# Gate and up projections of a SwiGLU layer by seven block products in place of eight

## The chip, the cores and the metric

The kernel runs on one core of a Trainium2 chip. The metric is the time of one execution on the device in microseconds (us); several executions are made and the median is taken.

## What is computed

Two layers of an encoder trunk, with the same weights for a batch of 512 tokens and one of 256, 768 tokens in all, of width 1024. Each layer has mixers (attention, retention, a recurrent group) and then the feed-forward part that this change touches. All of it is in float32:

```python
h = _rms(x, p['norm_ffn_pre'][l])
f = (jax.nn.silu(h @ p['ffn_w_gate'][l]) * (h @ p['ffn_w_up'][l])) @ p['ffn_w_down'][l]
x = x + _rms(f, p['norm_ffn_post'][l])
```

The inner width is D_FF = 2816, that is 22 feature tiles of 128.

## The kernel before

Every operand of a matmul is split into a high part (rounded to the matmul's format, float32r) and a low part, the rest. A product is then three matmuls: high by high, high by low, low by high. `hh` and `hl` hold the two parts of the normalised tokens, transposed: 8 blocks of 128 features by 768 tokens.

`piece` (L155) loads 128x1024 of weights into a `raw` buffer on SyncE's queue, writes the high part on ScalarE (L162) and the low part on VectorE or GpSimd in turn (L165). `feat_mm` (L181) multiplies the weights of one feature tile by a range of tokens: 8 blocks of the width by three matmuls (L189). Its columns are the tokens: 512 or 256.

`ffn` (L1239) goes through the 22 feature tiles in pairs (FFG = 2). For each tile `ffn_up` (L1189) makes the gate in the PSUM banks `pb` (`fg`) and the up projection in `pS` (`fu`), for both token ranges; tanh on ScalarE (L1197) and three steps on VectorE (L1198, L1217, L1220) give the activation, split into `ah` (L1219) and `al`. `ffn_down` (L1222) then takes both tiles at once: for each of six token tiles and two halves of the width, six matmuls of 512 columns into a `pa` bank (`dn`, L1231) and a sum into `y` on VectorE (L1237). The first pair goes by token ranges, and so does the last, whose down projection is followed tile by tile by the normalisation (`post_norm`, L218; `pre_norm`, L210, for the next layer).

All buffers come from pools with a tag and a fixed number of slots; a tile that finds no free slot waits until one is released:

```python
SLOTS = dict(raw=2, whi=3, wlo=3, E0=1, E1=1, E2=1, E3=1, E4=1, D=10, T=3, X=4, Z=2, z=2, V=2, Q=3, R=3, sm=2)
BANKS = dict(pa=2, pb=2, pS=2, pT=1, pO=1)
```

`R` slots hold 512 columns, `D` slots 768, `raw`, `whi`, `wlo` and `X` 1024. The order of the instructions on each engine is not the written one: a scheduler sets it when the program is built, by priority in the written order among what it finds ready. On the chip each engine then keeps that order and waits on semaphores.

Of the kernel before, what the change touches and what calls it, by code (L numbers as in the profile page):

```python
# [19 lines left out]
P = 128  # L20
L = 2
# [18 lines left out]
FFG = 2  # L40
# [18 lines left out]
FAST = (PIECE_D, PIECE_D + 2, PIECE_D + 6)  # L59
XM_TAG, XF_TAG = "ZXZXZX", "VZZVZZ"  # L60
# [22 lines left out]
class Trunk:  # L83
    def __init__(self, ctx, tc, xp, xs, wp, pv, bc, par, cst, scan, strips, yp, ys):
# [19 lines left out]
        self.nlo = 0  # L104
# [1084 lines left out]
    def ffn_up(self, l, f, seqs, wg, wu, th, ah, al):  # L1189
        nc = self.nc  # L1190
        part = len(seqs) < 2
        pg, pu = {}, {}

        def gate(s):
            t0, n, *_r = SEQS[s]
            c = slice(t0, t0 + n)
            nc.scalar.activation(th[:, c], pg[s][:, :n], AF.Tanh, scale=0.5)  # L1197
            nc.vector.scalar_tensor_tensor(out=th[:, c], in0=th[:, c], scalar=1.0, in1=pg[s][:, :n], op0=ALU.add, op1=ALU.mult)  # L1198

        for s in seqs:  # L1200
            pg[s] = self.bank("pS" if part else "pb", f"fg{l}_{f}_{s}")
            if not part:
                self.feat_mm(pg[s][:, :SEQS[s][1]], *wg, P, *SEQS[s][:2])
                gate(s)
        for s in seqs:
            t0, n, *_r = SEQS[s]
            c = slice(t0, t0 + n)
            pu[s] = self.bank("pS", f"fu{l}_{f}_{s}")
            if part:

                for a in range(0, n, 256):
                    self.feat_mm(pg[s][:, a:a + 256], *wg, P, t0 + a, 256)
                    self.feat_mm(pu[s][:, a:a + 256], *wu, P, t0 + a, 256)
                gate(s)
            else:
                self.feat_mm(pu[s][:, :n], *wu, P, t0, n)
            nc.vector.scalar_tensor_tensor(out=th[:, c], in0=th[:, c], scalar=0.5, in1=pu[s][:, :n], op0=ALU.mult, op1=ALU.mult)  # L1217
        c = slice(SEQS[seqs[0]][0], SEQS[seqs[-1]][0] + SEQS[seqs[-1]][1])
        nc.scalar.activation(ah[:, c], th[:, c], AF.Copy)  # L1219
        nc.vector.tensor_tensor(out=al[:, c], in0=th[:, c], in1=ah[:, c].bitcast(F32), op=ALU.subtract)  # L1220
# [18 lines left out]
    def ffn(self, l):  # L1239
# [4 lines left out]
        for f0 in range(0, NF, FFG):  # L1244
            fin = f0 + FFG >= NF
            tiles = [(self.tmp(f"th{l}_{f}"), self.slot("D", [P, TOK], f"ah{l}_{f}", F32R), self.slot("D", [P, TOK], f"al{l}_{f}", F32R))
# [209 lines left out]
```

## Time and profile before

| | |
|---|---|
| median of three runs (2332.1 to 2345.1) | 2338.31 us |
| profiled execution | 2336.97 us |
| its span, from the first to the last instruction | 2335.2 us |
| TensorE clock granted over the span, share of full | 0.979 |
| start of the first and the last gate matmul (`fg`) | 597.5 and 2307.6 us |
| start of the last down matmul (`dn`) of layer 0, of layer 1 | 1177.3 and 2324.5 us |
| DMA, mean over the span | 103 GB/s |

A row of a timeline has the start and the length in us, then the engine, the line and the operation with output<-inputs; in brackets stands how long the engine was idle before it, and what it waited for. PE is TensorE's matmul, PEld its weight load, DVE VectorE, ACT ScalarE, POOL GpSimd, SP SyncE. Matmuls overlap in their pipeline, so the distance of two starts, not the length, is what one costs in a row of them.

### The profile page before, as it was taken

To read this page: it belongs to the slowest core of one execution; us is meant where nothing else is said; L and a number is where in the kernel's file an instruction comes from. 1 tells how busy PE (TensorE), PEld (TensorE's weight loads), DVE (VectorE), ACT (ScalarE), POOL (GpSimd) and SP (SyncE) were. 2 spreads that over 40 slices of the span, in tenths; PEclk is the share of its full clock that TensorE was granted. 3 is DMA by queue.
4 is the path that set the end of the run, shared out by engine and by line. 5 is a ranking of instruction groups with operands and counts; after the bars stand their busy time and mean duration, and the time that the engine had idled before them with its cause. 6 is when DMAs were issued, how large, how long until landed. Compare 5 with 4: busy or idle time off the path is not lost.

```text
span 2335.2 us, 39824 instructions
## 1 busy us (share of the span) xinstructions
PE 2246.6 (96%) x15960; PEld 2028.8 (87%) x15960; DVE 1291.8 (55%) x2404; ACT 804.5 (34%) x1675; POOL 582.5 (25%) x521
## 2 busy tenths in 40 slices
PE   7999999999899999999999899999999999999997
PEld 7889999989888888888888799898898888888886
DVE  5598557885623333333567874678855343333345
ACT  4333335566431111221244333455654211222111
POOL 1342313325311111111233422133352111111113
PEclk9999999999999999999999899999999999999999
DMA  4543563335421111222324525633453111122112
GB/s 170 134 113 98 156 193 110 93 113 178 145 79 55 63 55 55 72 73 73 102 87 125 134 78 146 204 104 88 131 189 117 64 63 55 55 73 73 64 64 81
DMA packets 245080, 240.69 MB, mean 103 GB/s; under 512 B 138784, under 2 KB 191904, under 8 KB 244896
## 3 DMA queue, kind: packets, MB, share of 16 engines
q1 hardware_dynamic: 244896, 238.15, 33.2%
q8 instruction: 126, 2.06, 0.4%
q14 instruction: 58, 0.48, 0.1%
HBM read 183.03 MB, written 55.05 MB: 102 GB/s over the span
## 4 chain that ended last, share of the span: by engine, by line
PE 37%; DVE 7%; DMA 2%; issue 1%; ACT 1%; SPq 1%; POOL 1%; DVEq 0%; POOLq 0%; ACTq 0%
PE fg L189 8%; PE fu L189 8%; PE dn L1231 8%; PE dz L189 2%; PE op L178 2%; PE za L178 1%; PE zb L178 1%; PE pg L592 1%; DVE wlo L165 1%; PE px L575 1%; PE ob L766 1%; DMA raw<-in_wp_dram 1%; PE sd L537 1%; PE zc L178 1%; DVE nper L455 1%
## 5 line engine op out<-in xcount | busy, mean ns | idle before, releaser
L165 POOL TENSOR_TENSOR wlo<-raw,whi 128x1024 fp32r<-128x1024 f32 (+1 forms) x108 | 259.4, 2402 | 1034.9 <-ACT whi L162 854.7
L1237 DVE TENSOR_TENSOR y<-y,dn 128x512 f32<-128x512 f32 x240 | 162.7, 686 | 340.4 <-PE dn L1231 339.8
L162 ACT ACTIVATE whi<-raw 128x1024 fp32r<-128x1024 f32 (+1 forms) x222 | 225.3, 1021 | 334.3 <-DMA raw<-in_wp_dram 121.1
L189 PE MATMUL fg<-hh,whi 128*128 128x256 f32 (+1 forms) x768 | 250.4, 326 | 0.9 <-ACT hh L202 0.9
L189 PE MATMUL fg<-hl,whi 128*128 128x256 f32 (+1 forms) x768 | 250.4, 326 | 0.4 <-DVE hl L203 0.4
L189 PE MATMUL fg<-hh,wlo 128*128 128x256 f32 (+1 forms) x768 | 249.2, 325 | 0.0
L189 PE MATMUL fu<-hl,whi 128*128 128x256 f32 (+1 forms) x768 | 249.1, 324 | 0.0
L189 PE MATMUL fu<-hh,whi 128*128 128x256 f32 (+1 forms) x768 | 249.0, 324 | 0.0
L189 PE MATMUL fu<-hh,wlo 128*128 128x256 f32 (+1 forms) x768 | 248.4, 323 | 0.0
L165 DVE TENSOR_TENSOR wlo<-raw,whi 128x1024 fp32r<-128x1024 f32 (+1 forms) x114 | 154.6, 1356 | 128.8 <-ACT whi L162 127.8
L1231 PE MATMUL dn<-whi,ah 128*128 128x512 f32 x528 | 208.9, 396 | 1.9 <-DVE y L1237 1.9
L1231 PE MATMUL dn<-wlo,ah 128*128 128x512 f32 x528 | 209.4, 397 | 0.0
L1231 PE MATMUL dn<-whi,al 128*128 128x512 f32 x528 | 203.8, 393 | 0.0
L189 PEld LDWEIGHTS fg<-hh,whi 128*128 128x128 f32 x768 | 146.4, 191 | 16.1 <-ACT hh L202 1.3
L189 PEld LDWEIGHTS fg<-hl,whi 128*128 128x128 f32 x768 | 146.1, 190 | 15.1 <-DVE hl L203 1.0
L189 PEld LDWEIGHTS fu<-hl,whi 128*128 128x128 f32 x768 | 146.3, 190 | 13.6
L189 PEld LDWEIGHTS fu<-hh,wlo 128*128 128x128 f32 x768 | 146.1, 190 | 13.7
L189 PEld LDWEIGHTS fg<-hh,wlo 128*128 128x128 f32 x768 | 146.3, 190 | 13.4
L189 PEld LDWEIGHTS fu<-hh,whi 128*128 128x128 f32 x768 | 146.4, 191 | 13.1
L1219 ACT ACTIVATE ah<-th 128x768 fp32r<-128x768 f32 (+2 forms) x52 | 38.6, 742 | 297.6 <-DVE th L1217 297.6
L1197 ACT ACTIVATE th<-fg 128x512 f32<-128x512 f32 (+1 forms) x88 | 42.7, 485 | 234.8 <-PE fg L189 234.2
L1231 PEld LDWEIGHTS dn<-whi,al 128*128 128x128 f32 x528 | 98.7, 188 | 23.3
(358 smaller groups left out, 5586.6 us busy)
## 6 DMA issues: line engine op xcount, KB each, us to landing
raw<-in_wp_dram SPq DMA_DIRECT2D x184, 512.0 KB
raw<-in_wp_dram SPq DMA_DIRECT2D x38, 384.0 KB
kr<-kd SPq DMA_DIRECT2D x96, 64.0 KB
kr<-kd SPq DMA_DIRECT2D x48, 128.0 KB
x<-xm SPq DMA_DIRECT2D x24, 256.0 KB
xf<-x SPq DMA_DIRECT2D x12, 512.0 KB
gain<-in_bc_dram SPq DMA_DIRECT2D x8, 512.0 KB
bd<-sh SPq DMA_DIRECT2D x8, 512.0 KB
```

What stands on the lines that cost most here:

```text
L162: nc.scalar.activation(hi[:, :n], raw[:, :n], AF.Copy)
L165: eng.tensor_tensor(out=lo[:, :n], in0=raw[:, :n], in1=hi[:, :n].bitcast(F32), op=ALU.subtract)
L178: mm(ps, lhsT=a, rhs=b[:, c:c + ncol], start=i == 0, stop=i == tot - 1)
L189: mm(ps, lhsT=a, rhs=b, start=i == 0, stop=i == 3 * NK - 1)
L455: V.tensor_tensor(out=q[:, j + 1:32, 0:j], in0=q[:, j + 1:32, 0:j], in1=ev, op=ALU.add)
L537: T.matmul(psv[h][:, d, q], lhsT=bks[d][H[h], q], rhs=krs[d][H[h], h, q], start=True, stop=True)
L575: T.matmul(pxv[:, u], lhsT=krs[d][:, h, q], rhs=svs[d][:, h, q], start=True, stop=True)
L592: T.matmul(pgv[:, u], lhsT=brs[d][:, h, q], rhs=svs[d][:, h, q], start=True, stop=True)
L1197: nc.scalar.activation(th[:, c], pg[s][:, :n], AF.Tanh, scale=0.5)
L1219: nc.scalar.activation(ah[:, c], th[:, c], AF.Copy)
L1231: nc.tensor.matmul(ps, lhsT=a[p], rhs=w[q], start=i == 0, stop=i == tot - 1)
L1237: nc.vector.tensor_tensor(out=yt, in0=yt, in1=ps, op=ALU.add)
```

## The change

The first pair of feature tiles stays as it was, except that its down projection comes after both token ranges. For the other ten pairs of a layer, gate (and then up) of two feature tiles by 1024 by 768 tokens is seen as a 2x2 block product: the weights have two feature tiles by two halves of the width, the tokens two halves of the width by two halves of 384 tokens. Seven products of weight sums and token sums (Winograd's form of Strassen's product) take the place of eight block products, each of 4 blocks by three matmuls with 384 columns.

`ffn_sums` makes the token sums T1 to T4 once a layer, split into high and low parts, in buffers that other stages leave free (`TS_TAGS`); T1 overwrites a quarter of `hh` and `hl`. `block_weights` loads the two weight pieces, splits the first (w0) and the lower half of the second (w2, in `R`), lets GpSimd make four sums in place in `raw`, and splits these (wb, wa). `block_products` runs the seven products and adds them up on VectorE and GpSimd, with copies on ScalarE. `ffn_pair` does this for gate and up and makes the activation. The down projection of a pair is written behind the next pair's products, and that of the last pair comes after all, with its weights in `whi` and `wlo`.

```diff
-FFG = 2
+HT = TOK // 2
...
+TS_TAGS = ("Q", "T", "T", "T", "Z", "Z", "V", "D", "D", "Q", "Q")
...
-    def ffn_up(self, l, f, seqs, wg, wu, th, ah, al):
...
+    def ffn_sums(self, l):
+
+        nc = self.nc
+        V, S, A = nc.vector, nc.scalar, nc.gpsimd
+        F = lambda x: x.bitcast(F32)
+        L, R = slice(0, HT), slice(HT, TOK)
+        units = [self.slot(tag, [P, 2, HT], f"ts{l}_{i}", F32R) for i, tag in enumerate(TS_TAGS)]
+        cells = [u[:, j] for u in units for j in range(2)]
+        cells += [self.slot("z", [P, HT], f"tz{l}_{i}", F32R) for i in range(2)]
+        t1s = [self.tmp(f"t1{l}_{j}").rearrange("p (k c) -> p k c", k=2) for j in range(2)]
+        self.tt = {}
+        for k in range(4):
+            t1 = t1s[k // 2][:, k % 2]
+            t2, t3, t4 = [self.slot("R", [P, 512], f"t{n}{l}_{k}")[:, :HT] for n in (2, 3, 4)]
+            for eng, o, r, c in ((A, t1, k, L), (A, t3, k, R), (V, t2, 4 + k, R), (V, t4, 4 + k, L)):
+                eng.tensor_tensor(out=o, in0=F(self.hh[:, r, c]), in1=F(self.hl[:, r, c]), op=ALU.add)
+            A.tensor_tensor(out=t1, in0=t3, in1=t1, op=ALU.subtract)
+            A.tensor_tensor(out=t3, in0=t2, in1=t3, op=ALU.subtract)
+            V.tensor_tensor(out=t2, in0=t2, in1=t1, op=ALU.subtract)
+            V.tensor_tensor(out=t4, in0=t2, in1=t4, op=ALU.subtract)
+            for n, x in ((2, t2), (3, t3), (4, t4)):
+                hi, lo = cells.pop(0), cells.pop(0)
+                S.activation(hi, x, AF.Copy)
+                V.tensor_tensor(out=lo, in0=x, in1=F(hi), op=ALU.subtract)
+                self.tt[n, k] = hi, lo
+        for k in range(4):
+            t1, hi = t1s[k // 2][:, k % 2], self.hh[:, k, R]
+            S.activation(hi, t1, AF.Copy)
+            V.tensor_tensor(out=self.hl[:, k, R], in0=t1, in1=F(hi), op=ALU.subtract)
+
+    def block_h(self, n, k):
+
+        if n in (2, 3, 4):
+            return self.tt[n, k]
+        row, c = {1: (k, slice(HT, TOK)), "11": (k, slice(0, HT)), "21": (4 + k, slice(0, HT)), "22": (4 + k, slice(HT, TOK))}[n]
+        return self.hh[:, row, c], self.hl[:, row, c]
+
+    def block_mm(self, name, w, n):
+
+        mm = self.nc.tensor.matmul
+        ps = self.bank(("pb", "pb", "pS", "pS", "pT", "pO")[self.nbank % 6], name)[:, :HT]
+        self.nbank += 1
+        i = 0
+        for k in range(4):
+            wh, wl = [x[:, k * P:(k + 1) * P] for x in w]
+            bh, bl = self.block_h(n, k)
+            for a, b in ((wh, bh), (wh, bl), (wl, bh)):
+                mm(ps, lhsT=a, rhs=b, start=i == 0, stop=i == 11)
+                i += 1
+        return ps
+
+    def block_weights(self, l, f, i):
+
+        nc = self.nc
+        V, S, A = nc.vector, nc.scalar, nc.gpsimd
+        F = lambda x: x.bitcast(F32)
+        H = slice(0, 512), slice(512, 1024)
+        raw = []
+        for j in range(2):
+            r = self.slot("raw", [P, 1024], f"raw{l}_{f + j}_{i}")
+            nc.sync.dma_start(out=r, in_=self.wp[l, PIECE_FF + 3 * (f + j) + i])
+            raw.append(r)
+        a, b = raw
+        nm = f"{l}_{f}_{i}"
+
+        def split(hi, lo, x):
+            S.activation(hi, x, AF.Copy)
+            V.tensor_tensor(out=lo, in0=x, in1=F(hi), op=ALU.subtract)
+            return hi, lo
+
+        pair = lambda n: [self.slot(tag, [P, 1024], f"w{n}{nm}_{j}", F32R) for j, tag in enumerate(("whi", "wlo"))]
+        w0 = split(*pair("a"), a)
+        w2 = split(*[self.slot("R", [P, 512], f"w{n}2{nm}", F32R) for n in "hl"], b[:, H[1]])
+
+        A.tensor_tensor(out=b[:, H[1]], in0=b[:, H[0]], in1=b[:, H[1]], op=ALU.add)
+        A.tensor_tensor(out=b[:, H[0]], in0=a[:, H[0]], in1=b[:, H[0]], op=ALU.subtract)
+        A.tensor_tensor(out=a[:, H[0]], in0=b[:, H[1]], in1=a[:, H[0]], op=ALU.subtract)
+        A.tensor_tensor(out=a[:, H[1]], in0=a[:, H[1]], in1=a[:, H[0]], op=ALU.subtract)
+        wb = split(*pair("c"), b)
+        wa = split(*pair("b"), a)
+        part = lambda w, j: tuple(x[:, H[j]] for x in w)
+        return {"A11": part(w0, 0), "A12": part(w0, 1), "A22": w2, "S1": part(wb, 1), "S2": part(wa, 0), "S3": part(wb, 0), "S4": part(wa, 1)}
+
+    def block_products(self, l, f, i, w, out):
+
+        V, A = self.nc.vector, self.nc.gpsimd
+        (c11, c12), (c21, c22) = [(o[:, :HT], o[:, HT:]) for o in out]
+        add = lambda eng, o, x, y, op=ALU.add: eng.tensor_tensor(out=o, in0=x, in1=y, op=op)
+        copy = lambda o, x: self.nc.scalar.activation(o, x, AF.Copy)
+        p = lambda n, wn, hn: self.block_mm(f"p{n}{l}_{f}_{i}", w[wn], hn)
+        copy(c11, p(1, "A11", "11"))
+        p2 = p(2, "A12", "21")
+        p3 = p(3, "S4", "22") if f == 2 else None
+        add(V, c12, c11, p(6, "S2", 2))
+        add(V, c11, c11, p2)
+        add(V, c21, c12, p(7, "S3", 3))
+        copy(c22, p(5, "S1", 1))
+        add(A, c12, c12, c22)
+        add(A, c22, c21, c22)
+        p3 = p3 or p(3, "S4", "22")
+        add(V, c12, c12, p3)
+        add(V, c21, c21, p(4, "A22", 4), ALU.subtract)
+
+    def ffn_pair(self, l, f):
+
+        nc = self.nc
+        V, S = nc.vector, nc.scalar
+        g, th = [[self.tmp(f"{n}{l}_{f + j}") for j in range(2)] for n in ("fz", "ft")]
+        w = self.block_weights(l, f, 0)
+        self.block_products(l, f, 0, w, g)
+
+        for j in range(2):
+            S.activation(th[j], g[j], AF.Tanh, scale=0.5)
+            V.scalar_tensor_tensor(out=g[j], in0=th[j], scalar=1.0, in1=g[j], op0=ALU.add, op1=ALU.mult)
+        u = [self.tmp(f"fy{l}_{f + j}") for j in range(2)]
+        w = self.block_weights(l, f, 1)
+        self.block_products(l, f, 1, w, u)
+        out = []
+        for j in range(2):
+            V.scalar_tensor_tensor(out=g[j], in0=g[j], scalar=0.5, in1=u[j], op0=ALU.mult, op1=ALU.mult)
+            hi, lo = [self.slot("D", [P, TOK], f"{n}{l}_{f + j}", F32R) for n in ("ah", "al")]
+            S.activation(hi, g[j], AF.Copy)
+            V.tensor_tensor(out=lo, in0=g[j], in1=hi.bitcast(F32), op=ALU.subtract)
+            out.append((hi, lo))
+        return out
...
+    def ffn_up(self, l, f, s, wg, wu, th, ah, al):
...
-        for f0 in range(0, NF, FFG):
-            fin = f0 + FFG >= NF
...
+        down_w = lambda f0, tags=("X", "X"): [self.piece(l, PIECE_FF + 3 * f + 2, tags=tags) for f in range(f0, f0 + 2)]
+
+        tiles = [(self.tmp(f"th{l}_{f}"), self.slot("D", [P, TOK], f"ah{l}_{f}", F32R), self.slot("D", [P, TOK], f"al{l}_{f}", F32R)) for f in range(2)]
+        ws = []
+        for f in range(2):
+            ws.append([self.piece(l, PIECE_FF + 3 * f + i, tags=("Q", "Q") if f and i else ("whi", "wlo")) for i in range(2)])
+            self.ffn_up(l, f, 0, *ws[f], *tiles[f])
+        for f in range(2):
+            self.ffn_up(l, f, 1, *ws[f], *tiles[f])
+        self.ffn_sums(l)
+        wd = down_w(0)
+        act = [t[1:] for t in tiles]
+        for t in range(NT):
+            self.ffn_down(l, 0, t, act, wd)
+
+        act = None
+        for f0 in range(2, NF, 2):
+            fin = f0 + 2 >= NF
+            before, act = act, self.ffn_pair(l, f0)
+            if before:
+                wd = down_w(f0 - 2)
+                for t in range(NT):
+                    self.ffn_down(l, f0 - 2, t, before, wd)
+            if not fin:
+                continue
+            wd = down_w(f0, ("whi", "wlo"))
+            g_post, g_next = (*self.gains(l, 3), None) if last else self.gains(l, 3, 4)
+            for s in (1, 0):
...
+                for t in range(SEQS[s][2], SEQS[s][2] + SEQS[s][3]):
+                    self.ffn_down(l, f0, t, act, wd)
...
```

## Rows read from the trace of the kernel before

**Rows 1.** The page's first part: busy us, share of the span, instructions
```profile
PE 2246.6 (96%) x15960; PEld 2028.8 (87%) x15960; DVE 1291.8 (55%) x2404; ACT 804.5 (34%) x1675; POOL 582.5 (25%) x521
```

**Rows 2.** Stretches: length, then each engine's busy us, clock, DMA share, GB/s
```profile
core 0: us, PE busy (x) PEld busy (x) DVE busy (x) ACT busy (x) POOL busy (x), PEclk, DMA share, GB/s
597.00:610.00 13.00, 8.17 (x67) 7.58 (x65) 13.00 (x14) 6.63 (x11) 11.48 (x7) 1.00 0.40 136
610.00:620.00 10.00, 9.43 (x55) 9.13 (x56) 6.84 (x13) 4.26 (x7) 2.19 (x3) 0.66 0.86 297
...
840.00:890.00 50.00, 50.00 (x265) 42.77 (x264) 17.83 (x25) 9.66 (x12) 7.73 (x3) 1.00 0.19 63
```

**Rows 3.** TensorE in order of time: start us, length us, line, operation
```profile
689.66 0.39 PE L189 MATMUL fu<-hh,whi 128*128 128x512 f32 x1
...
691.70 0.28 PE L189 MATMUL fu<-hh,whi 128*128 128x256 f32 x1
...
694.45 0.28 PE L189 MATMUL fu<-hh,wlo 128*128 128x256 f32 x1
...
705.75 0.39 PE L189 MATMUL fu<-hh,whi 128*128 128x512 f32 x1
705.99 0.40 PE L1231 MATMUL dn<-whi,ah 128*128 128x512 f32 x1
...
708.78 0.40 PE L189 MATMUL fu<-hl,whi 128*128 128x512 f32 x1
```

**Rows 4.** VectorE in order of time, one pair of feature tiles
```profile
835.16 1.22 DVE L165 TENSOR_TENSOR wlo<-raw,whi 128x1024 fp32r<-128x1024 f32 x1
...
853.72 1.29 DVE L1237 TENSOR_TENSOR y<-y,dn 128x512 f32<-128x512 f32 x2 [4.46 <-PE dn L1231]
...
884.85 0.69 DVE L1237 TENSOR_TENSOR y<-y,dn 128x512 f32<-128x512 f32 x1 [0.20 <-PE dn L1231]
885.45 1.22 DVE L165 TENSOR_TENSOR wlo<-raw,whi 128x1024 fp32r<-128x1024 f32 x1
```

**Rows 5.** Groups with shapes: ns minimum/median/maximum, first and last start
```profile
L165 DVE TENSOR_TENSOR wlo<-raw,whi x114: 945/1225/2643, 12.6 to 2288.8; 128x1024 fp32r<-128x1024 f32 x95, 128x768 fp32r<-128x768 f32 x19
...
L162 ACT ACTIVATE whi<-raw x222: 832/1059/1071, 10.5 to 2287.7; 128x1024 fp32r<-128x1024 f32 x92, 128x768 fp32r<-128x768 f32 x19
...
L225 POOL TENSOR_TENSOR yg<-y,gain x40: 1268/1296/2290, 556.3 to 2327.7; 128x512 f32<-128x512 f32 x40
...
L1197 ACT ACTIVATE th<-fg x88: 362/481/601, 619.5 to 2308.2; 128x512 f32<-128x512 f32 x44, 128x256 f32<-128x256 f32 x44
L1198 DVE SCALAR_TENSOR_TENSOR th<-th,fg x88: 406/548/690, 620.2 to 2308.8; 128x512 f32<-128x512 f32 x44, 128x256 f32<-128x256 f32 x44
```

**Rows 6.** SyncE's weight loads and the ScalarE step that waits for one
```profile
836.40 12.34 SPq L158 DMA_DIRECT2D raw<-in_wp_dram  x5
...
840.03 1.06 ACT L162 ACTIVATE whi<-raw 128x1024 fp32r<-128x1024 f32 x1 [2.34 <-DMA raw<-in_wp_dram]
```

**Rows 7.** GpSimd and VectorE steps that overlap in time, both in time order
```profile
642.74 2.40 POOL L165 TENSOR_TENSOR wlo<-raw,whi 128x1024 fp32r<-128x1024 f32 x1 [21.07 <-ACT whi L162]
643.00 2.42 DVE L1220 TENSOR_TENSOR al<-th,ah 128x256 fp32r<-128x256 f32 x1 [0.91 <-ACT ah L1219]
...
835.70 2.93 POOL L165 TENSOR_TENSOR wlo<-raw,whi 128x1024 fp32r<-128x1024 f32 x1 [25.70 <-ACT whi L162]
...
857.90 2.40 POOL L165 TENSOR_TENSOR wlo<-raw,whi 128x1024 fp32r<-128x1024 f32 x1 [11.40 <-ACT whi L162]
858.46 0.69 DVE L1237 TENSOR_TENSOR y<-y,dn 128x512 f32<-128x512 f32 x1
```

**Rows 8.** VectorE as the tokens are normalised, before the stage and after it
```profile
621.91 1.29 DVE L203 TENSOR_TENSOR hl<-hT,hh 128x512 fp32r<-128x512 f32 x2 [0.27 <-ACT hh L202]
...
1185.14 1.41 DVE L226 SCALAR_TENSOR_TENSOR xf<-yg,q3r,xf 128x512 f32<-128x512 f32 x2
...
1190.59 1.32 DVE L203 TENSOR_TENSOR hl<-hT,hh 128x512 fp32r<-128x512 f32 x2
```

More of the change, by code (lines that the diff above doesn't have):

```diff
@@ L103, in __init__ @@
         self.hl = G.tile([P, NK, TOK], F32R, name="hl")
-        self.nlo = 0
+        self.nlo = self.nbank = 0
     def slot(self, tag, shape, name, dt=F32):
@@ L1186, in mixers @@
                     (START, 1.0, self.out(l)), (START, DENSE_RATE, self.op(l))])
-    def ffn_up(self, l, f, seqs, wg, wu, th, ah, al):
+    def ffn_sums(self, l):
         nc = self.nc
[L1191 to L1218, printed above, removed]
@@ new lines, in ffn_up @@
+    def ffn_up(self, l, f, s, wg, wu, th, ah, al):
+        nc = self.nc
+        t0, n, *_r = SEQS[s]
+        c = slice(t0, t0 + n)
+        pg, pu = self.bank("pS", f"fg{l}_{f}_{s}"), self.bank("pS", f"fu{l}_{f}_{s}")
+        for a in range(0, n, 256):
+            self.feat_mm(pg[:, a:a + 256], *wg, P, t0 + a, 256)
+            self.feat_mm(pu[:, a:a + 256], *wu, P, t0 + a, 256)
+        nc.scalar.activation(th[:, c], pg[:, :n], AF.Tanh, scale=0.5)
+        nc.vector.scalar_tensor_tensor(out=th[:, c], in0=th[:, c], scalar=1.0, in1=pg[:, :n], op0=ALU.add, op1=ALU.mult)
+        nc.vector.scalar_tensor_tensor(out=th[:, c], in0=th[:, c], scalar=0.5, in1=pu[:, :n], op0=ALU.mult, op1=ALU.mult)
@@ new lines, in ffn @@
+        for f in range(2):
[18 more added lines that the diff above has]
+            for s in (1, 0):
+                late = None
+                for t in range(SEQS[s][2], SEQS[s][2] + SEQS[s][3]):
+                    self.ffn_down(l, f0, t, act, wd)
+                    x = self.slot(XF_TAG[t], [P, DM], f"xf{l}_{t}")
+                    nc.sync.dma_start(out=x, in_=self.x1[t])
+                    if last:
+                        dst = self.yp[0, t * P:(t + 1) * P, :] if t < 4 else self.ys[0, (t - 4) * P:(t - 3) * P, :]
+                    else:
+                        dst = self.xd[t]
+                    self.post_norm(self.y[t], x, t, g_post, True, dst)
+                    if not last:
+                        if late:
+                            self.pre_norm(*late, g_next)
+                        late = x, t
```

32 lines of the change are left out of this document (removed).

## The prediction

> **What bounds the kernel now.** First the busy shares of the whole span: TensorE (PE) 96%, VectorE (DVE) 55%, ScalarE (ACT) 34%, GpSimd (POOL) 25% [rows 1]. A share is a mean over stages, so the table of stretches comes next: in 50 us out of the middle of the feed-forward stage PE is busy for all 50.00, at a granted clock of 1.00, DVE for 17.8, ACT for 9.7 and POOL for 7.7 [rows 2]. PE is the limit there and the others have room. Since matmul records overlap, what a matmul takes is read from the distance of the starts [rows 3]: from 689.66 to 691.70 lie 9 distances of 512 columns, 0.227 each; from there to 694.45 lie 23 of 256 columns, 0.1196 each; twelve matmuls of the down projection (512 columns) lie between 705.99 and 708.78, 0.233 each.
>
> One pair of feature tiles has 96 up and gate matmuls of 512 columns, 96 of 256, and 72 down: 96 x 0.227 + 96 x 0.1196 + 72 x 0.233 = 21.8 + 11.5 + 16.8 = 50.1 us. The same DVE instruction comes back after 885.45 - 835.16 = 50.29 us [rows 4], so 0.2 us of a pair is lost at most. This stage runs on its count of matmul columns.
>
> **Removed.** Ten pairs a layer, twenty in all, get seven products of 12 matmuls with 384 columns for each of gate and up: 168 in place of 192. No row has 384 columns; its bounds are 0.1196 and 0.227. Between the two the distance grows by 0.107 for 256 columns, and 384 lies in the middle: I take 0.173. Then 168 x 0.173 = 29.1 against 33.3, that is 4.15 us a pair and **83 us** in 20 pairs. The down matmuls stay as they are.
>
> **Added in each pair.** Durations are from the groups [rows 5]: splitting 1024 columns takes 1.06 on ACT and 1.22 on DVE (medians), 768 columns 0.83 and 0.95 (the minima); 512 columns take 1.28 on POOL; DVE reading PSUM takes 0.41 for 256 and 0.69 for 512 columns (the ends), so 0.55 for 384, ACT 0.36 and 0.60, so 0.48; POOL's 384 are scaled to 1.0, and its 1024 take 2.40 [rows 7].
> - DVE: 7 weight splits (3.5 for each projection) 8.5, 10 product sums 5.5, 4 gate and up steps and 2 splits of 768 columns 5.7, 12 down sums of 0.69 8.3, one down weight 1.2: 29 us, where it was 17.8.
> - POOL: 8 weight sums 10.2, 4 product sums 4, one down weight 2.4: 17 us. ACT: 7 splits 7.4, 4 copies 1.9, tanh and splits 3.3, two down weights 2.1: 15 us.
> - DMA: the same six pieces of 512 KB on SP's queue.
>
> With PE at 46.1 (29.1 + 16.8 + 0.2) none of these is the limit by its sum. All are priced at nothing while PE has other work; the chain below is what happens where it has none.
>
> **The chain of weight sums.** Half of the second tile's weights (w2) is split into two of only three R buffers, so one of them waits until the last product of the projection before (the one with A22) has read it. POOL's four in-place sums wait for that split, since they overwrite what it reads; then come wb and wa. From the end of that product: 0.69 (DVE, 512) + 4 x 1.28 + 1.06 + 1.22 = 8.1 us to wa. PE has only products 1 and 2 meanwhile, 24 x 0.173 = 4.15. From up to the next gate the down projection, 16.8 us, covers the rest. From gate to up nothing in program order does, so up to 4.0 us lie open per pair. If wb's products go first, the chain is 0.69 + 2 x 1.28 + 1.06 + 1.22 = 5.5 and 1.4 lie open; if the A22 product itself, which needs only w2, is drawn ahead of the others, its buffers come back early and nothing does. Which it is depends on the order that the scheduler writes out. In the kernel before it takes what is ready: one matmul of an up projection at 705.75, twelve of a down projection, then the up projection again [rows 3]. So the written order won't stand, and I take the middle case, 1.5 us a pair: **+30 us**, bounds 0 and 4.0 (80 us).
>
> The raw pieces are held longer, through all four sums. One lands 3.6 us after its issue (840.03 - 836.40) [rows 6], and with two buffers the next projection's pieces are called as wb and wa are split, some 10 us before they are needed: nothing, bounds 0 and 1 us a pair, the latter in the range. SP's queue keeps its order, so down weights come behind the pair's own and are ready as up ends. D keeps eight of its ten buffers, two hold token sums; the next gate's first copy then waits until the down projection has given back four. Down sums are spread over 31 us of a pair now (853.72 to 884.85) [rows 4]; six PSUM banks let as many products run ahead, so I price it at nothing too.
>
> **Two engines, one port.** Where POOL computes on SBUF, a DVE step with two SBUF operands stands still: a split of 256 columns, as many as take 0.41 from PSUM [rows 5], takes 2.42 at 643.00, just after POOL began 2.40 us of its own, and ends just after it; the other way round POOL takes 2.93 at 835.70, where DVE began 0.54 before it [rows 4]; a DVE sum with one PSUM operand at 858.46 stays at 0.69 under POOL [rows 7]. The pair now has 15.4 us of such DVE steps (8.5 + 5.7 + 1.2) and 17 us of POOL, 32 in turn, in 46. By the mean of these rows a meeting costs half a microsecond to two; one or two a pair on the chain are in the 1.5 above.
>
> The Trainium skill, "SBUF — State Buffer", section "Who interferes with whom", says that this is an exclusive lock held for a whole instruction, not a shared rate, and that whoever issues first wins. The 2.42 us row agrees. By that rule every meeting on the chain costs up to a full POOL step, which is the third rival below.
>
> **Head and tail.** Once a layer the token sums take 16 POOL steps (16 us) and 32 DVE steps of 384 columns at 0.55 (17.6 us), 33.6 in turn. They need the normalised tokens, whose last part is written at 623.2 [rows 8], and end near 657; the first weights' chain behind them, 8.1, ends near 665. PE has until then the rest of the first pair (33.3 less 8.17 + 9.43 [rows 2] and some 3 until 623: 13 us), its down projection (16.8) and three products (6.2): to about 659. I take 5 us a layer, **+10**; bounds 0 and 12 a layer. The layer's end had two tiles' normalisation under matmuls and now has none, but a whole down projection (16.8) comes in their place at the point where the end used to wait for DVE (steps of 0.7 for each half tile, 1.41 and 1.32 in pairs [rows 8]): nothing, bounds -5 and +8.
>
> **Sum**: -83 + 30 + 10 = -43 us. The profiled execution took 2336.97 us, 1.3 less than the median of the runs, 2338.31; from there 2294.
>
> **Rivals.**
> - *All hidden* (13%): the scheduler draws the A22 product ahead and every chain is covered, 2337 - 83 + 5 = 2259. For it: PE never idle in the stage and 17 us of slack on DVE. Against it: POOL and DVE alternate on the chain.
> - *The written order, slower* (14%): each up projection waits for wa behind its two products, 4.0 plus one held port of 0.5, 4.5 a pair, 90 us: -83 + 90 + 10 = +17, 2354. It decides from (83 - 10) / 20 = 3.65 us a pair. For it: the R buffers, which the code shows; against it: the interleaving in rows 3. The clock would add to it: after 13 us in which PE was busy 8.17, the next 10 were granted 0.66 [rows 2].
> - *The port* (13%): chain steps meet whole POOL steps, 1.5 + 1.28 + 0.5 = 3.3 a pair, 66: -83 + 66 + 10 = -7, 2330. For it: the 2.42 us row; against it: the sums in PSUM, half of DVE's new work, are not touched.
> - *No shorter matmul* (4%): 384 columns take what 512 do, 168 x 0.227 = 38.1 against 33.3: +96 without any stall, 2433. Seven products would then not be less work. 256 columns at half the time of 512 speak against it.
>
> **Chances.** The forecast has 56%: from stalls of 0.5 a pair and 4 us for the heads (-83 + 10 + 4, 2268) to 2.7 a pair and 10 (-83 + 54 + 10, 2318). The range 2262 to 2348 leaves out the upper half of the written order, the last rival and a part of the first, some 17%. A measurement of this kernel tells about 0.5%, 11.7 us, from no change. Faster than that: the forecast, all hidden and a part of the port, 0.72; the same: most of the port and the low end of the written order, 0.12; slower 0.16.
>
> **What would show it.** In the profile after: matmuls of 384 columns 0.173 apart; a pair's period near 48; PE idle of about 1.5 us between gate and up, its releaser a wa or wb split; DVE at 29 of 48. Wrong would be: a distance above 0.18; A22 products last and a wait over 3.6 us a pair; a granted clock below 1.00 in the steady stage; down matmuls that start late for their weights; PE waiting over 12 us for the token sums.

## The result, and the profile after

The changed kernel takes 2423.19 us (median; 2415.3 to 2426.4), the kernel before in the same session 2338.8: a ratio of 1.0356, 95% interval 1.0318 to 1.0394. It is slower by 3.6%, where 2294 was forecast; the time lies above the range.

The page's first part after the change (columns as in [rows 1]):

```profile
PE 2221.6 (92%) x15288; PEld 2041.5 (84%) x15288; DVE 1615.7 (67%) x2704; ACT 916.9 (38%) x1823; POOL 877.6 (36%) x753
```

TensorE has 672 matmuls fewer than in [rows 1] (24 in each of 18 pairs, and 120 in the last pair of each layer, where before all tokens went 256 at a time) and is busy for 25 us less, in a span that is 89 us longer (2424.5 against 2335.2). So the work did shrink, and what grew is the time in which TensorE waits or runs slowly. The table of stretches says where (columns as in [rows 2]):

```profile
core 0: us, PE busy (x) PEld busy (x) DVE busy (x) ACT busy (x) POOL busy (x), PEclk, DMA share, GB/s
640.00:700.00 60.00, 54.29 (x297) 49.21 (x295) 41.02 (x54) 25.73 (x45) 30.32 (x24) 1.00 0.12 36
700.00:1100.00 400.00, 363.58 (x1785) 329.85 (x1786) 243.30 (x275) 111.58 (x138) 158.65 (x99) 0.95 0.19 58
1163.00:1253.00 90.00, 73.33 (x426) 63.05 (x425) 65.97 (x96) 33.66 (x53) 32.17 (x29) 0.94 0.36 119
```

Between 700 and 1100 us, where the kernel before had TensorE full at a clock of 1.00 [rows 2], it now stands still for 36.4 of 400 us and was granted 0.95. How long a pair takes is read on ScalarE from the tanh of the gates, eight pairs apart:

```profile
718.42 1.58 ACT L1305 ACTIVATE ft<-fz 128x768 f32<-128x768 f32 x2 [6.30 <-DVE fz L1280]
...
1142.91 0.85 ACT L1305 ACTIVATE ft<-fz 128x768 f32<-128x768 f32 x1 [4.07 <-DVE fz L1280]
```

(1142.91 - 718.42) / 8 = 53.06 us a pair, against 50.29 [rows 4] and 47.6 forecast. TensorE at the turn from one pair's gate to its up projection, in order of time. In the names of tiles, `wh` and `wl` are the A22 weights; `wa` holds A11 and A12; `wc` is the variable `wb` of the code (S1, S3) and `wb` the variable `wa` (S2, S4):

```profile
873.30 0.40 PE L1343 MATMUL dn<-whi,al 128*128 128x512 f32 x1
873.59 0.61 PE L1240 MATMUL p<-ts,wh 128*128 128x384 f32 x2
...
876.14 0.51 PE L1240 MATMUL p<-hh,wa 128*128 128x384 f32 x2
...
879.78 0.34 PE L1240 MATMUL p<-hh,wa 128*128 128x384 f32 x1
883.20 1.01 PE L1240 MATMUL p<-ts,wc 128*128 128x384 f32 x2 [3.08 <-ACT wc L1259]
...
885.98 3.57 PE L1240 MATMUL p<-ts,wc 128*128 128x384 f32 x10 [1.13 <-DVE wc L1260]
889.34 0.72 PE L1240 MATMUL p<-hh,wc 128*128 128x384 f32 x2
```

Three things are to be seen. From 876.14 to 879.78 lie 21 distances of 384 columns, 0.173 each: the size on which the 83 us rest is right. The gate's A22 product runs last, at 873.59, behind the whole down projection. And then TensorE has only the up projection's first two products; it waits 3.08 and 1.13 us for the split of `wc`, and its next ten matmuls are 3.36 / 10 = 0.336 us apart, half speed. This turn is like the others: between 700 and 1130 us, eight pairs, the waits for the split of `wc` make 30.0 of TensorE's 39.2 us.

The same stretch on ScalarE, in order of time:

```profile
862.70 0.63 ACT L1259 ACTIVATE wh<-raw 128x512 fp32r<-128x512 f32 x1 [3.54 <-DMA raw<-in_wp_dram]
873.04 0.95 ACT L1281 ACTIVATE fz<-p 128x384 f32<-128x384 f32 x2 [9.71 <-PE dn L1343]
```

On GpSimd, where L1280 are the gate's product sums and L1267 and L1268 the first two weight sums of up and L1270 the fourth:

```profile
876.03 1.35 POOL L1280 TENSOR_TENSOR fz<-fz,fz 128x384 f32<-128x384 f32 x1 [20.42 <-DVE fz L1280]
877.34 1.29 POOL L1267 TENSOR_TENSOR raw<-raw 128x512 f32<-128x512 f32 x1
878.58 1.02 POOL L1280 TENSOR_TENSOR fz<-fz 128x384 f32<-128x384 f32 x1
879.56 1.99 POOL L1268 TENSOR_TENSOR raw<-raw,raw 128x512 f32<-128x512 f32 x1
...
882.97 1.87 POOL L1270 TENSOR_TENSOR raw<-raw 128x512 f32<-128x512 f32 x1
```

And on VectorE:

```profile
875.82 0.69 DVE L1260 TENSOR_TENSOR wl<-raw,wh 128x512 fp32r<-128x512 f32 x1
...
881.85 1.85 DVE L1306 SCALAR_TENSOR_TENSOR fz<-ft,fz 128x768 f32<-128x768 f32 x1 [0.97 <-ACT ft L1305]
883.63 2.29 DVE L1260 TENSOR_TENSOR wc<-raw,wc 128x1024 fp32r<-128x1024 f32 x1
```

The gate's first copy out of PSUM (`fz<-p`) starts at 873.04; the profile puts the 9.71 us before it down to the down projection, whose end gives D buffers back. The high part of the up projection's A22 weights (`wh`) is there from 863.3 on, the low part (`wl`) only at 875.82, right behind the gate's A22 product, which frees an R buffer. Then come the weight sums on GpSimd (L1267, L1268), with one of the gate's own product sums (L1280) ahead of each, and the split of `wc`. From the A22 product's end (875.8, where the next product starts) to that of the split (885.92) are 10.1 us, and two products cover 4.1 of them. Between 700 and 1130 us the list of waits (us, times, longest) has the copy's as the largest on ScalarE:

```profile
ACT fz L1281 <- PE dn L1343: 74.1, 7, 12.3
```

### The profile page after: what moved, and what is told of

The parts are those of the page before. It is cut to its first block, busy times and chain, and to the rows that moved or that the text cites. A ratio compares the mean times of both kernels' runs of the same rounds, so it can differ in the third digit from the quotient of the medians.

```text
span 2424.5 us, 39277 instructions
## 1 busy us (share of the span) xinstructions
PE 2221.6 (92%) x15288; PEld 2041.5 (84%) x15288; DVE 1615.7 (67%) x2704; ACT 916.9 (38%) x1823; POOL 877.6 (36%) x753
## 4 chain that ended last, share of the span: by engine, by line
PE 48%; DVE 25%; DMA 10%; issue 6%; POOL 5%; ACT 5%; SPq 1%; DVEq 0%; POOLq 0%; ACTq 0%
PE p L1240 10%; PE dn L1343 9%; DMA raw<-in_wp_dram 6%; PE dz L191 4%; PE za L180 3%; PE zb L180 2%; PE op L180 2%; DVE wc L1260 2%; DVE fz L1280 2%; DVE el L455 2%; PE sd L539 1%; DVE wlo L167 1%; PE pg L594 1%; DVE nper L457 1%; PE ob L768 1%
## 5 line engine op out<-in xcount | busy, mean ns | idle before, releaser
L167 POOL TENSOR_TENSOR wlo<-raw,whi 128x1024 fp32r<-128x1024 f32 (+1 forms) x68 | 158.5, 2331 | 309.0 <-ACT whi L164 285.2
L1240 PE MATMUL p<-ts,wc 128*128 128x384 f32 x480 | 123.5, 398 | 61.5 <-ACT wc L1259 38.2
L1240 PE MATMUL p<-hh,wa 128*128 128x384 f32 x640 | 171.7, 338 | 6.4 <-ACT wa L1259 3.0
L1240 PEld LDWEIGHTS p<-ts,wc 128*128 128x128 f32 x480 | 101.0, 226 | 75.0 <-ACT wc L1259 42.4
L1280 POOL TENSOR_TENSOR fz<-fz,fz 128x384 f32<-128x384 f32 x20 | 27.7, 1383 | 341.0 <-DVE fz L1280 341.0
L1240 PEld LDWEIGHTS p<-hh,wa 128*128 128x128 f32 x640 | 116.9, 189 | 11.6 <-ACT wa L1259 4.5
L180 PE MATMUL zc<-whi,hh 128*128 128x256 f32 x384 | 114.9, 301 | 3.6 <-DVE u L259 1.8
L1343 PEld LDWEIGHTS dn<-wlo,ah 128*128 128x128 f32 x528 | 100.9, 191 | 19.3 <-POOL wlo L167 0.9
L180 PE MATMUL zc<-wlo,hh 128*128 128x256 f32 x384 | 113.3, 296 | 0.3 <-DVE wlo L167 0.2
L180 PE MATMUL zc<-whi,hl 128*128 128x256 f32 x384 | 113.4, 296 | 0.0
L1240 PE MATMUL p<-hl,wa 128*128 128x384 f32 x320 | 108.0, 338 | 0.0
```

Of the source, the lines that this page charges most:

```text
L167: eng.tensor_tensor(out=lo[:, :n], in0=raw[:, :n], in1=hi[:, :n].bitcast(F32), op=ALU.subtract)
L180: mm(ps, lhsT=a, rhs=b[:, c:c + ncol], start=i == 0, stop=i == tot - 1)
L1240: mm(ps, lhsT=a, rhs=b, start=i == 0, stop=i == 11)
L1280: add = lambda eng, o, x, y, op=ALU.add: eng.tensor_tensor(out=o, in0=x, in1=y, op=op)
L1343: nc.tensor.matmul(ps, lhsT=a[p], rhs=w[q], start=i == 0, stop=i == tot - 1)
```

## The experiments

The theory to test (A): D is short, so the gate's copy, and with it the A22 product, comes last; so R comes back late, and the up projection's weight chain lies open. Against it (B): that chain is simply too long, in any order. And (C): the R buffers alone hold it up, because A22 is written last, whatever D does. Ratios are to the kernel before on the same chip, with 95% intervals. Differences of times from different chips are good to some 5 us: the kernel before took 2333.1 to 2338.8 on them.

**1. Two D buffers given back.** The token sums T3 and T4 of k = 2 have no tiles; their products read those of k = 1, so the results are not the reference's.

```diff
-TS_TAGS = ("Q", "T", "T", "T", "Z", "Z", "V", "D", "D", "Q", "Q")
+TS_TAGS = ("Q", "T", "T", "T", "Z", "Z", "V", "Q", "Q")
...
+                if k == 2 and n > 2:
+                    self.tt[n, k] = self.tt[n, 1]
+                    continue
```

> The token sums give back their two D buffers, so that all ten serve the pairs (two of the four third and fourth token sums' blocks are those of another block; which part is left out: T3 and T4 of the third block are not made, T3 and T4 of the second stand in). Theory A, the D buffers: in the changed kernel the gate's first product cannot be copied out before the down projection of the pair before has given back its buffers, six banks fill, the seventh product (A22) comes last, its R buffers come back late and the weight sums of up lie open. Without it the 7 us of PE idle in a pair fall to about 2, the period from 53 to about 48, the time from 2423 to about 2325. Theory B, the weight chain itself (GpSimd and VectorE one at a time, raw buffers): it lies open whatever D does, 2405 to 2423. Theory C, the R buffers alone, since A22 is written last: 2405 to 2423.

2324.49 us, ratio 0.9963 [0.9942, 0.9985]. Ten buffers in place of eight for the pairs' tiles are worth 99 us, although A22 is still written last: theory A had 2325, B and C had no gain. No wait of the gate's copy on the down projection is left in the steady part, only 1.84 us of the tanh behind it, and a pair takes (1104.37 - 814.85) / 6 = 48.3 us:

```profile
814.85 1.56 ACT L1308 ACTIVATE ft<-fz 128x768 f32<-128x768 f32 x2
...
1104.37 1.58 ACT L1308 ACTIVATE ft<-fz 128x768 f32<-128x768 f32 x2 [1.84 <-PE dn L1346]
```

**2. The A22 product written third.** Its sum stays last.

```diff
         p2 = p(2, "A12", "21")
+        p4 = p(4, "A22", 4)
...
-        add(V, c21, c21, p(4, "A22", 4), ALU.subtract)
+        add(V, c21, c21, p4, ALU.subtract)
```

> The A22 product is written third, behind the two of w0, so that its R buffers come back early; D stays as it is. Theory C: the wait of up for its weight sums goes, 2325 or so. Theory A: the copy of the gate still waits for the down projection, but the chain of up starts earlier: half of the gain, 2360 to 2390. Theory B: 2405 to 2423.

2319.0 us, ratio 0.9925 [0.9896, 0.9954], and every result is computed. A pair takes (1101.34 - 765.00) / 7 = 48.0 us; TensorE is busy for 292.57 of the 300 us from 800 on, at a clock of 1.00. It gives more than expected under A (2360 to 2390) and comes out near what C had, which experiments 1 and 4 rule out. With the product early, the shortage of D costs less, but not nothing: without it, in experiment 3, the kernel is 31 us faster.

**3. Both.** T3 and T4 of k = 2 are left out as in 1.

> Both edits together (T3 and T4 of the third block left out as in the run that frees D). Theory A: little more than the freed D buffers alone, 2310 to 2325. Theory C: the same as A22 third alone. Theory B: 2400 or more.

2288.22 us, ratio 0.9812 [0.9756, 0.9868]. TensorE is busy for 297.60 of the 300 us from 800 on, and a pair takes (1078.87 - 848.37) / 5 = 46.1 us, the 29.1 + 16.8 + 0.2 of the prediction. All weight sums are still there, so rival B falls: the chain is hidden once its start is early enough. It is 22 us below what A had. Either edit alone gives back some 100 us and both 135: with one of the two causes left, only 31 to 36 us remain.

**4. The down projection written between gate and up.** The activations of the pair before are then read before the pair's own are written, so D holds one pair's less. `between()` writes that down projection; its definition, which the cut leaves out, is the loop that stood behind the pair.

```diff
         w = self.block_weights(l, f, 0)
         self.block_products(l, f, 0, w, g)
...
+        between()
         u = [self.tmp(f"fy{l}_{f + j}") for j in range(2)]
         w = self.block_weights(l, f, 1)
```

> The down projection of the pair before is written between the gate's and the up's products and no longer behind both; all is computed. Theory A: the buffers come back before up needs its own, and the down projection covers up's weight chain; what opens is the chain of the next gate, now without cover: a part of the gain, 2340 to 2380. Theory B: the chain is as long, only elsewhere, 2400 to 2423. Theory C: the chain lies under the down projection for up and open for the next gate, no gain, 2400 to 2423.

2311.96 us, ratio 0.9909 [0.9885, 0.9934]: with every result computed and A22 still written last, this order is worth 111 us, more than A had (2340 to 2380). The gate's copy no longer waits for the down projection. But the down projection now also stands ahead of the up products and can cover their weight chain, so this run does not tell what the shortage alone is worth. Pairs take some 49.7 and 44.8 us in turn, (1053.24 - 769.54) / 6 = 47.3 on average.

**5. Fixed buffers.** The pairs' tiles are taken once a layer.

```diff
-        g, th = [[self.tmp(f"{n}{l}_{f + j}") for j in range(2)] for n in ("fz", "ft")]
+        g, u, ab = self.fixed
+        th = u
...
+        self.fixed = g, u, ab
```

> Edit: the gate, up and activation tiles of the pairs lie in eight D buffers that are taken once a layer and written again pair by pair, and the tanh goes into the tile that later takes the up result; nothing is left out and the products keep their written order, the A22 product as the last. Theory A (the gate's first copy of the changed kernel waits for D buffers that the pool hands back only as the down projection of the pair before ends; so the banks stay full, the A22 product runs last, its R buffers come free late and the up weights' chain lies open): the gate's results no longer share buffers with what the down projection reads, the down projection's matmuls fall among the products of gate and up, and a pair falls from 53.1 us to 46 to 48; 2285 to 2330 us. Rival B (the weight chain is too long by itself and is in the way in any order): a pair stays above 51 us; over 2390. Rival D (one set of buffers ties each pair to the end of the pair before, a new wait of the gate's first copy on the activation split, some 5 us a pair): 2400 to 2450.

2344.48 us, ratio 1.0041 [1.0025, 1.0058]. One thing in the expectation is wrong: a down projection is written behind the next pair's products, so it reads the activations that the next pair has put into the fixed tiles, and has to wait for them. The results are not the reference's, and the kernel says nothing on rival D; experiment 10 asks again.

**6. The order of the tail.** In the last pair only tiles 4 and 5 of the down projection of 18 and 19 run ahead.

```diff
-                for t in range(NT):
+                for t in (4, 5) if fin else range(NT):
                     self.ffn_down(l, f0 - 2, t, before, wd)
...
-            wd = down_w(f0, ("whi", "wlo"))
+            wd, wb = down_w(f0, ("whi", "wlo")), wd
...
+                    if s == 0:
+                        self.ffn_down(l, f0 - 2, t, before, wb)
                     self.ffn_down(l, f0, t, act, wd)
```

> Edit: in the last pair of each layer only tiles 4 and 5 of the down projection of features 18 and 19 run ahead; for tiles 0 to 3 it comes tile by tile, right ahead of that of features 20 and 21. Nothing is left out. Theory T (at the end of each layer the six normalisations start only when the down projections of 18 and 19 have run through, so about 15 us a layer lie in the tail, which the prediction priced at nothing): the first normalisation starts eight half-tile products earlier, 8 x 1.40 = 11 us; VectorE still has six of them, so 6 to 11 us a layer come back: 2400 to 2412 us. Rival (VectorE is full from the end of the products on, and its own work of six normalisations sets the end): within 4 us of the changed kernel, 2419 to 2427.

2417.94 us, ratio 1.0349 [1.0323, 1.0375], not clearly different from the changed kernel's, and between the ranges of theory T and of its rival. Inconclusive; see 12 and 13.

**7. No weight sums.** The lines L1267 to L1270 are taken out.

> Edit: the four sums and differences of weight blocks on GpSimd are left out (the splits read the raw blocks), so the results are not the reference's; the products, their order as written and all splits stay. Theory A: the chain behind the R buffers loses four operations of 1.3 to 2.2 us, 6 to 7 us together, and the two or three products that stand ready at the start of up cover what is left; the A22 product still runs last, but a pair falls by 4 to 6 us to 47 to 49: 2310 to 2350 us. Rival E (what a pair loses is the wait of the gate's first copy itself, and the chain lies beside it): a pair stays above 51 us, over 2390. VectorE's weight splits, 2.29 us beside GpSimd's sums in the changed kernel, should all be near 1.23 here.

2299.68 us, ratio 0.9847 [0.9816, 0.9877]. Leaving out four GpSimd steps in each projection is worth 123 us, 6.2 a pair, 10 us more than A had at best; a pair takes (1086.14 - 749.76) / 7 = 48.1 us. The gate's A22 product comes as late as before:

```profile
888.20 0.62 PE L1240 MATMUL p<-ts,wh 128*128 128x384 f32 x2
```

The weight split that took 2.29 us takes 1.22 here, and it runs 11 us ahead of that product:

```profile
876.94 1.22 DVE L1260 TENSOR_TENSOR wc<-raw,wc 128x1024 fp32r<-128x1024 f32 x1 [2.49 <-ACT wc L1259]
```

So rival E falls. But the 123 us are not the length of the four steps alone: without sums that overwrite the raw block, the split of `wc` need not wait for `wl` and its R buffer either.

**8. Fixed buffers, A22 third, tail.** The edits of 5, 2 and 6, with the fault of 5.

> Edit: fixed buffers, the A22 product written third, and the tail's order, all three; nothing is left out. Theory A with T: TensorE has no idle time in the steady part, a pair takes 192 x 0.234 = 44.9 us less 24 x (0.234 - 0.174) ... that is 72 down products at 0.234 and 168 block products at 0.174, 46.1 us; the third kernel's 2288 less 6 to 11 us a layer: 2266 to 2278 us. Rival B: over 2390. If only the tail's order fails: 2285 to 2292.

2342.64 us, ratio 1.0034 [1.0016, 1.0053], as 5. The fault hides what was asked.

**9. Between, and A22 third.** The edits of 4 and 2; `between()` stands a line later than in 4, behind the tiles of the up projection. Every result is computed.

> Edit: the down projection of the pair before is written between the gate's and the up's products (as in the fourth experiment), and the A22 product third (as in the second); nothing is left out. Theory A (what costs the time is that the A22 product comes last; it comes last because the gate's first copy finds all D buffers taken while the down projection of the pair before waits behind the next pair's products, and because it is written last): with both causes gone as in the third experiment, but with every result computed, a pair takes 46 us and the whole 2285 to 2300 us. Rival F (written between, the down projection can no longer fill the gap behind the up products, where the activation's chain runs, so a part of the gain goes back): no better than the better of its two halves, 2308 to 2320 us.

2285.24 us, ratio 0.9782 [0.9762, 0.9802]. It beats both kernels, the one before by 2.2%. TensorE is full in the steady part, by the table of stretches (columns as above):

```profile
800.00:1100.00 300.00, 300.00 (x1560) 278.80 (x1559) 195.18 (x240) 93.33 (x117) 126.51 (x85) 1.00 0.24 73
```

A pair takes (1039.35 - 809.03) / 5 = 46.06 us by the gates' tanh on ScalarE, and rival F falls:

```profile
809.03 0.85 ACT L1306 ACTIVATE ft<-fz 128x768 f32<-128x768 f32 x1 [3.35 <-DVE fz L1280]
...
1039.35 0.85 ACT L1306 ACTIVATE ft<-fz 128x768 f32<-128x768 f32 x1 [2.84 <-DVE fz L1280]
```

**10. The ninth, with fixed buffers.** Here each down projection stands ahead of the next pair's activations.

> Edit: as the ninth, and the gate, up and activation tiles lie in eight fixed D buffers that each pair writes again; the down projection that reads the activations is written ahead of the next pair's, and nothing is left out. Theory A: with the down projection written between, D is no longer short, so it matters nothing which of its buffers is used: within 6 us of the ninth. Rival D (a pool that hands its buffers around costs something by itself): faster than the ninth by over 10 us.

2292.59 us, ratio 0.9824 [0.981, 0.9837]: 7.4 us slower than the ninth, a little more than the 6 that A allows, where rival D had it over 10 us faster. Once D is no longer short, it is not the handing round of buffers that costs.

**11. R buffers of its own for the up projection's A22 weights.** D stays short and A22 last; T3 and T4 of k = 2 are left out as in 1, to make room (the cut shows the new buffers alone).

```diff
-        w2 = split(*[self.slot("R", [P, 512], f"w{n}2{nm}", F32R) for n in "hl"], b[:, H[1]])
+        w2 = split(*[self.slot(t, [P, 512], f"w{n}2{nm}", F32R) for n, t in zip("hl", ("TQ" if i else "RR"))], b[:, H[1]])
```

> Edit: the up projection's A22 weights (both parts) get a T and a Q buffer of their own in place of R, so the gate's A22 product no longer holds them up; for this the token sums T3 and T4 of k = 2 are left out (their products read those of k = 1), so the results are not the reference's. D stays as short as in the changed kernel, and the A22 product is still written last. Theory A with R as its link (the up weights' sums on GpSimd, which overwrite the raw block, wait for the split of A22's weights, that split waits for an R buffer, and that for the gate's A22 product): the sums run during the down projection, the up products S1 to S4 find their weights ready, and a pair falls by 4 to 6 us to 47 to 49: 2310 to 2350 us, although the gate's first copy waits for D as long as before and the A22 product of the gate still comes behind the down projection. Rival Q (GpSimd works in order, and the gate's product sums, which wait for the gate's copy, stand ahead of the weight sums; or the D wait itself is what a pair loses): a pair stays at 51 to 53, over 2390 us.

2303.68 us, ratio 0.9858 [0.9836, 0.988], 6 us below the range of A; a pair takes (1098.67 - 816.27) / 6 = 47.07 us. The gate's copy and its A22 product come as late as before, but the weight sums run 20 us ahead of them. The gate's copy on ScalarE, in order of time:

```profile
904.46 0.86 ACT L1284 ACTIVATE fz<-p 128x384 f32<-128x384 f32 x2
```

The down projection and then the gate's A22 product on TensorE:

```profile
904.60 0.50 PE L1346 MATMUL dn<-whi,ah 128*128 128x512 f32 x1 [0.21 <-ACT whi L164]
904.99 0.62 PE L1243 MATMUL p<-ts,wh 128*128 128x384 f32 x2
```

The up projection's A22 weights, split on VectorE:

```profile
882.36 0.69 DVE L1263 TENSOR_TENSOR wl<-raw,wh 128x512 fp32r<-128x512 f32 x1 [0.83 <-ACT wh L1262]
```

And the first of its weight sums on GpSimd:

```profile
883.13 1.95 POOL L1270 TENSOR_TENSOR raw<-raw 128x512 f32<-128x512 f32 x1 [6.08 <-DVE wl L1263]
```

`wl` is split as soon as `wh` is there. So the link is the R buffer: the late copy and the late A22 product by themselves leave a pair within 1 us of the 46.1 of experiment 3, and that half of rival Q falls which takes the wait for D itself to be the loss. Its other half is not settled: with the buffers free, the scheduler also wrote the weight sums ahead of the gate's product sums on GpSimd, and no run tells what that order alone is worth.

**12 and 13. The changed kernel and the tail's order, on one chip.**

> Edit: none, the changed kernel itself, timed on the same chip as the thirteenth, to compare the two directly. Both theories: 2415 to 2427 us, ratio to before near 1.036.

> Edit: the kernel of the sixth experiment again (last pair: the down projection of 18 and 19 of tiles 0 to 3 comes tile by tile right ahead of that of 20 and 21), beside the changed kernel on one chip. Theory T: in the sixth experiment's trace the stretch from the last pair's gate to the next layer's first sums was 99.2 us where the changed kernel has 110.3, and the last layer's end was 8.4 us shorter, 19 us together; the median moved by only 5, since a stage that the edit doesn't touch began 6 us later in that profile. On one chip the whole should be 12 to 20 us shorter than the twelfth. Rival (what the tail gives is taken back in the next layer's mixers, which start earlier but finish no earlier): within 7 us of the twelfth.

2423.23 us, ratio 1.0384 [1.0358, 1.0411], and 2412.15 us, ratio 1.0332 [1.031, 1.0354]: 11 us between them, short of theory T's 12 and beyond its rival's 7. Five marks in each trace, in order of time: the first layer's last gate, the next layer's first sums of squares, that layer's first gate, its last gate, the last step of all. The changed kernel:

```profile
1143.20 0.85 ACT L1305 ACTIVATE ft<-fz 128x768 f32<-128x768 f32 x1 [4.09 <-DVE fz L1280]
...
1251.97 0.72 PE L328 MATMUL kn<-cs,ksq 128*128 128x2 f32 x6
...
1814.90 0.60 ACT L1328 ACTIVATE th<-fg 128x512 f32<-128x512 f32 x1 [2.08 <-PE fg L191]
...
2290.35 0.85 ACT L1305 ACTIVATE ft<-fz 128x768 f32<-128x768 f32 x1 [4.09 <-DVE fz L1280]
...
2415.10 1.41 DVE L228 SCALAR_TENSOR_TENSOR xf<-yg,q3r,xf 128x512 f32<-128x512 f32 x2 [0.66 <-POOL q3r L153]
```

The tail's order:

```profile
1139.73 0.85 ACT L1305 ACTIVATE ft<-fz 128x768 f32<-128x768 f32 x1 [4.09 <-DVE fz L1280]
...
1241.68 0.95 PE L328 MATMUL kn<-cs,ksq 128*128 128x2 f32 x8
...
1815.85 0.60 ACT L1328 ACTIVATE th<-fg 128x512 f32<-128x512 f32 x1 [1.86 <-PE fg L191]
...
2291.91 0.85 ACT L1305 ACTIVATE ft<-fz 128x768 f32<-128x768 f32 x1 [4.09 <-DVE fz L1280]
...
2408.74 1.41 DVE L228 SCALAR_TENSOR_TENSOR xf<-yg,q3r,xf 128x512 f32<-128x512 f32 x2 [0.81 <-POOL q3r L153]
```

The first tail is 1251.97 - 1143.20 = 108.8 against 102.0 us, but the mixers behind it take 562.9 against 574.2, and the second feed-forward stage begins 1 us later than without the edit. Behind the second tail, 124.8 against 116.8 to the start of its last step, comes nothing, and its 8 us are kept. So each theory holds at one of the two places, in these two traces, which differ by 6.5 us (2421.64 and 2415.16), not by the 11 of the medians. In the mixers TensorE stands still for 29.7 us against 24.8 and is busy for 6.2 us longer; what causes it stays open.

## Why the prediction was wrong

**What bounds the kernel, and what is removed: right.** 384 columns are 0.173 apart, a full pair takes 46.1 us (experiments 3 and 9), and 20 x (50.29 - 46.1) = 84 us are gone from TensorE's work. The rival without a shorter matmul falls.

**D priced at nothing: the step that failed.** It read "the next gate's first copy then waits until the down projection has given back four … six PSUM banks let as many products run ahead, so I price it at nothing too". The wait came, and the seventh product, for which no bank is left, is A22, the very one whose R buffers the up projection's weight chain needs. I had costed the chain and the buffers apart. Experiments 1 and 4 remove the shortage (4 by an order that also covers the chain), 2 takes the product out of its reach, 11 cuts the link at R; each gives back 99 to 120 us. Among what would show it wrong the prediction named this picture, A22 products last and a wait over 3.6 us a pair.

**The chain of weight sums: mis-sized for that reason.** Priced at 1.5 us a pair, since "the written order won't stand"; interleaving in the kernel before [rows 3] was the evidence, but it does not show what the scheduler does when a buffer is missing. The rival of the written order, at 14%, was right that up waits for the chain behind its two products, though it waits for the variable wb (`wc`) and not for wa; its price was too small: 4.5 us, with 4.0 open. Measured are 53.06 - 46.1 = 7.0 a pair, 139 us in 20. Of these TensorE stands still for 36.4 x 53.06 / 400 = 4.8; the other 2.1 lie in matmuls at half speed, 14 in the pair shown, by an estimate 14 x (0.336 - 0.173) = 2.3, which its text mentioned (the 0.66 of [rows 2]) but did not add. The chain to `wc` took 10.1 us, not 5.5: a product sum of the gate stands ahead of each of the two weight sums on GpSimd, and L1268 and the split of `wc` were lengthened, 1.99 and 2.29 us for 1.28 and 1.22. Even the upper bound, 4.0, was thus too low, which let the range end at 2348.

**The port: right in kind, and inside the failed term.** The split of `wc` ran into L1270 (882.97 to 884.84) and ended 1.08 us after it; without sums it takes 1.22 (experiment 7). The Trainium skill, "SBUF — State Buffer", section "Who interferes with whom", says that the two engines lock each other out for whole instructions; these rows agree. As a rival by itself (3.3 us a pair) the port falls: the sums are all still there in experiments 3 and 9, which lose nothing by them.

**Raw pieces, down weights, sums of each engine's load: nothing, as priced.** With all of them in place TensorE is full in experiment 9.

**The head: right in size, for other waits.** 5 us a layer forecast; TensorE stands still for 5.7 of the 60 us between 640 and 700. But it does not wait for the first weights' chain behind the token sums. The largest item is the first pair's down projection, which waits for ScalarE's copies, and these stand behind splits of token sums (us, times, longest):

```profile
PE dn L1343 <- ACT y L1347: 2.9, 2, 1.8
```

That the size came out is thus in part luck.

**The tail: wrong.** Priced at nothing, bounds -5 and +8. From the last gate or up product to the next layer's first sums of squares there were 54.0 us before:

```profile
1154.33 0.28 PE L189 MATMUL fu<-hh,wlo 128*128 128x256 f32 x1
...
1208.36 0.95 PE L326 MATMUL kn<-cs,ksq 128*128 128x2 f32 x8
```

and 90.1 after, from the matmul right behind the last product:

```profile
1163.09 0.40 PE L1343 MATMUL dn<-whi,ah 128*128 128x512 f32 x1
...
1253.17 0.72 PE L328 MATMUL kn<-cs,ksq 128*128 128x2 f32 x6
```

One of the three groups of down matmuls in these stretches, before and after:

```profile
L1231 PE MATMUL dn<-whi,ah 128*128 128x512 f32 x16 | 6.5, 406 | 0.0
```

```profile
L1343 PE MATMUL dn<-whi,ah 128*128 128x512 f32 x48 | 20.1, 423 | 6.3 <-DVE y L1349 4.7 <-DVE q5r L152 1.5
```

In all three there are 144 where there were 48: the 72 of features 18 and 19, and 24 of features 20 and 21 for tiles 4 and 5, which before ran ahead of the last up matmul. They account for 96 x 0.233 = 22.4 of the difference; 13.7 us remain, and TensorE stands still for 16.7 us where it did for 6.2. The step took it that the down projection of 18 and 19 would fill the place of the two lost overlapped normalisations. It does delay all six, and VectorE is busy for 65.97 of these 90 us. That VectorE, with one normalisation after the other, sets the rest is likely but not shown.

**The sum**, by what was measured: -84 + 139 + 34 = +89 us, the 34 (17 a layer) not measured but what is left for both ends and for pairs that lose less than a middle one. In the ninth kernel the 139 are gone: -84 + 34 = -50, and its span is 50.1 us shorter than that of before (2285.1 against 2335.2).

## What to carry to other kernels

When a change makes a buffer wait possible, ask which instruction is the first to find nothing left, and what its own buffers are wanted for; a wait that looks covered can hold the start of a chain that is not. Write the product that others wait for early, and its consumer late. The price of a chain is that of its start as well as its length: taking eight weight sums a pair out gives back 123 us in an order where a late buffer holds their start, while in another order, with all of them in place, TensorE has no idle time in the steady part.

## What the runs showed of the hardware that was not expected

In the changed kernel short waits cost twice. After 3.08 and 1.13 us without work, ten matmuls came 0.336 us apart, at the lower of TensorE's two clocks (1.2 of 2.4 GHz). The granted clock was 1.00 from 870.00 to 879.90 and 0.96 in the first wait, up to 883.20; then it was 0.50, and it rose again after these ten matmuls (0.96 from 889.30 to 895.00):

```profile
883.20:884.90 1.70, 1.64 (x4) 1.13 (x4) 1.70 (x2) 0.03 (x1) 1.64 (x1) 0.50 0.00 0
...
886.00:889.30 3.30, 3.30 (x10) 3.30 (x11) 1.19 (x1) 0.00 (x0) 0.00 (x0) 0.50 0.67 186
```

Over the steady part it was 0.95. In experiments 2 and 7 TensorE waited too, 7.4 and 6.9 us in 300, and the granted clock stayed at 1.00.
